# Float16 pairs for layer 1's projections and forgetting-attention logits, with scales from weight bounds gathered in layer 0

## The chip, the core and the metric

One NeuronCore of a Trainium2 chip runs the whole program. The metric is device time in microseconds (us) of one execution, as the median of three. Names of the engines as the profile has them: PE is the matrix engine, PEld its weight loads, DVE the vector engine, ACT the scalar engine, POOL GpSimd, SP the engine whose queue issues all of this kernel's DMAs.

## What is computed

A decoder trunk of two layers over 1024 tokens of width 1024. Layer 0 mixes by causal pooling, layer 1 by forgetting attention; both add a 4-head cross-attention into 256 memory tokens, and both end in an output projection and a LayerNorm.

```python
def mixer_sublayer(x, mem, w_in, w_mem_kv, w_out, main_fn):
    h = x @ w_in                      # 1024 -> 3072: main | mem q | main gate | mem gate
    y_main = main_fn(u_main)
    y_mem = memory_attention(q_mem, mem, w_mem_kv)
    y = concat([y_main * silu(g_main), y_mem * silu(g_mem)])
    return y @ w_out

# layer 1's main_fn; k, v, cum come from one projection of layer 0's output
logits = einsum('bqhd,bkhd->bhqk', qi, k) * FOX_HEAD_DIM ** -0.5
logits = logits + (ci[..., :, None] - cum_k[:, :, None, :])     # causal
p = softmax(logits);  out = einsum('bhqk,bkhd->bqhd', p, v)

x = layer_norm(ALPHA * x + y, ln_g, ln_b)
```

Everything is float32 at the interface: 16 heads of width 64, sequence 1024, in blocks of 128 queries.

## The kernel before

**Three products for one.** To keep float32 accuracy, `hi_lo` (L159) splits an operand into three tiles: `hi`, the value rounded to the 4-byte type fp32r, by ACT (L162); `lo`, the remainder in bfloat16, by DVE (L163); and `top`, the value in bfloat16, by ACT (L164). A product `a*b` is then hi·hi in fp32r plus top·lo and lo·top in bfloat16 (`three`, L153). When `low[0]` is set, in the main loop of the forgetting attention, `gp_hi_lo` (L166) makes a weight's three tiles on POOL instead.

**A slab** (`slab`, L193) is the projection to 128 output channels: two weight pieces of 128x512, each loaded by SP into one of four `raw` buffers and split into two of six `w` buffers (`hi` in one, the pair `lo`/`top` in the other), then 48 matmuls with 512 moving columns (L214): 16 in fp32r and 32 in bfloat16, in two accumulators, each evacuated after its 24th matmul. Layer 0 has 24 slabs and layer 1 has 38.

**Layer 0.** `pool_group(0)`, then `mem_attention` (four slabs of memory queries, after each of which the memory's keys and values of one head are projected by `mem_kv`, L248; then ten rounds, each with one block of memory logits and softmax, and with parts of four gate slabs put between them), then `pool_group(1)` to `(3)`, each with four slabs. `OutProj.rest` (L457) multiplies by `w_out` (L441); `norm` (L481) normalizes 128 rows at a time, and PE transposes them (L294) into `X1`, which `hi_lo` splits into layer 1's `X`.

**Layer 1.** The memory keys (L248) and `mem_attention` again, then `v_first` (L643: the first values and the forget logits, with X as the stationary operand, L657), the forget gates, whose cumulated logs `cum` go through a DRAM line `cumd`, and the main loop `fox` (L873). It goes over 16 heads and, in a head, from the longest block of queries (1024 keys) to the shortest (128). Of each block: POOL masks a part of the row `R` of `cum` (L773); PE makes the logits with two fp32r matmuls for each stretch of up to 512 keys (L191, into three banks `L`); DVE adds `R` and takes the running minimum (L781); ACT takes the exponential (L789); DVE and ACT make the sums' inverse and two float16 halves of the probabilities (L799 to L811); a DMA transposes them (L824), and five rounds later PE multiplies by the values (L833). For the logits, a head's keys lie in one tile as `hi` on 64 partitions and `lo` on the other 64, with a second tile `ws` that has the two swapped by DMA (L716), so that two matmuls over 128 partitions give all four products.

**Order.** PE's order in the main loop is written by hand (`manual_schedule`): `Fill` holds the slabs of the next pairs and gates, and `pump` puts a share of their matmuls between a block's logits and its values, so that slabs are spread evenly over the rounds. All other engines run in the order in which a planner, which follows the text's order as its priority, has put their instructions, each engine one after the other. The planner also gives out the buffers: a load into `raw` waits for the splits that read the buffer's last content, and a split waits for the slab's matmuls that read the `w` buffer's last content.

```python
    def hi_lo(to, src, pinned=False, top=None):
        pin = tc.keep_in_program_order if pinned else lambda ins: ins
        pin(nc.scalar.copy(to.hi, src))
        pin(nc.vector.tensor_tensor(to.lo, src, to.hi.bitcast(F32), ALU.subtract))
        (top or nc.scalar.copy)(to.top, src)
```

## Time and profile before

| | |
|---|---|
| median of three runs | 1219.38 us (1218.32 to 1220.52) |
| the profiled execution | 1218.15 us, of which the profile's span is 1216.4 us |
| granted PE clock | 0.997 of full speed |
| layer 0 up to its output projection | 0 to 330 us of the span |
| output projection, norm and transposes of layer 0 | 330 to 463 us |
| memory keys of layer 1; its memory attention, first values | 463 to 482 us; 482 to 658 us |
| main loop of the forgetting attention | 658 to 1076 us |
| output projection and norm of layer 1 | 1076 to 1216 us |

The stages are read from where each line's matmuls begin and end. Two things are needed to read the rows. A matmul's row gives a mean of 380 ns, which is the time from its start to the modelled arrival of its last result; the next one starts much earlier, so the distance between two starts is what counts, and it comes from a stretch with its count. And a windows row gives, for each engine, busy microseconds with the number of instructions in brackets, then the granted clock, the mean busy share of the 16 DMA engines, and GB/s.

### The profile page before, as it was taken

The numbers are of one execution on the slowest core, as the hardware profiler recorded it, in microseconds if no ns is written. First come the engines' busy times: TensorE is split into PE (matmuls) and PEld (weight loads), VectorE is DVE, ScalarE is ACT, GpSimd is POOL, SyncE is SP. The second block draws the span as 40 slices with busy tenths as digits, with TensorE's granted clock in tenths as the row PEclk, the third lists the DMA queues.
The fourth block names the chain that finished last, engine by engine and source line by source line (L and its number), as shares of the span: only waits on it lengthen the run. The fifth ranks groups of instructions, "written<-read, shape, count | busy, mean of one in ns | idle before, by whom it ended". The sixth has DMA issues, their size and how long they took to land. (4 is left out here: it accounts for less than half of the span.)

```text
span 1216.4 us, 20026 instructions
## 1 busy us (share of the span) xinstructions
PE 1193.7 (98%) x7018; PEld 758.7 (62%) x7018; DVE 793.3 (65%) x1853; ACT 697.4 (57%) x1474; POOL 221.0 (18%) x349
## 2 busy tenths in 40 slices
PE   9999999999999998999999999999999999999996
PEld 4566666555555666667686666666666666665553
DVE  7534676475644457357736888878877888874754
ACT  6556774374542345567533777767776777685220
POOL 4000000000000000000002454544444434640000
PEclk9999999999999999999999999999999999999999
DMA  6232553232452333234517879988887989895340
GB/s 229 84 112 95 122 131 139 95 121 88 164 182 104 111 129 116 70 96 109 159 52 181 162 161 194 181 187 172 182 195 159 193 188 229 222 241 195 132 156 36
DMA packets 267414, 178.68 MB, mean 147 GB/s; under 512 B 212272, under 2 KB 225712, under 8 KB 267312
## 3 DMA queue, kind: packets, MB, share of 16 engines
q1 hardware_dynamic: 267312, 177.40, 56.2%
q8 instruction: 55, 0.90, 0.3%
q14 instruction: 47, 0.39, 0.1%
HBM read 94.97 MB, written 22.61 MB: 97 GB/s over the span
## 5 line engine op out<-in xcount | busy, mean ns | idle before, releaser
L214 PE MATMUL pj<-A,w 128*128 128x512 bf16 (+1 forms) x2928 | 684.7, 390 | 3.1 <-DVE B L724 1.6
L214 PEld LDWEIGHTS <-w 128*128 128x128 bf16 x1984 | 182.3, 98 | 223.8 <-issue 23.3
L214 PEld LDWEIGHTS pj<-A,w 128*128 128x128 f32 x976 | 181.1, 189 | 45.8 <-ACT A L162 2.8
L789 ACT ACTIVATE T<-MK,s 128x512 f32<-128x512 f32 x192 | 111.3, 580 | 41.5 <-DVE s L781 23.6
L811 DVE SCALAR_TENSOR_TENSOR P<-T,s,P 128x512 f16<-128x512 f32 x192 | 111.6, 613 | 34.7 <-ACT P L810 33.4
L163 DVE TENSOR_TENSOR w<-raw,w 128x512 bf16<-128x512 f32 x106 | 75.6, 714 | 83.6 <-PE pj L214 51.5
L810 ACT ACTIVATE P<-T,s 128x512 f16<-128x512 f32 x192 | 103.0, 576 | 46.0 <-ACT T L789 20.1
L441 PEld LDWEIGHTS <-T 128*128 128x128 bf16 x736 | 70.7, 98 | 82.9 <-issue 3.7
L191 PE MATMUL L<-B,B 128*128 128x512 f32 (+3 forms) x384 | 105.8, 381 | 2.2 <-DVE s L781 2.1
L686 POOL MEMSET G<- 128x128 f32 x1 | 0.2, 208 | 581.5 <-ACT MK L164 581.5
L191 PEld LDWEIGHTS L<-B,B 128*128 128x128 f32 x384 | 70.8, 189 | 22.9 <-DVE s L781 4.8
L162 ACT CAST w<-raw 128x512 fp32r<-128x512 f32 x106 | 65.9, 621 | 26.6 <-PE pj L214 14.6
L157 POOL TENSOR_SCALAR w<-raw 128x512 fp32r<-128x512 f32 x108 | 67.3, 629 | 65.0 <-PE pj L214 59.7
L781 DVE CUSTOM_DVE_ANT_0 MK<-L,R 128x512 f32<-128x512 f32 (+3 forms) x128 | 72.5, 566 | 8.7 <-PE L L191 6.9
L164 ACT CAST w<-raw 128x512 bf16<-128x512 f32 x106 | 65.7, 620 | 18.9 <-PE pj L214 18.2
L773 POOL TENSOR_SCALAR_AFFINE_SELECT R<-R 128x128 f32<-128x128 f32 x128 | 41.3, 328 | 174.4 <-DVE s L781 129.4
L168 POOL TENSOR_TENSOR w<-raw,w 128x512 bf16<-128x512 f32 x54 | 69.6, 1288 | 18.7 <-PE pj L214 16.2
L163 DVE TENSOR_TENSOR T<-T,T 128x1024 bf16<-128x1024 f32 x23 | 28.0, 1218 | 52.2 <-ACT T L162 36.9
L833 PE MATMUL O<-T,V 128*64 128x128 f16 (+1 forms) x1152 | 57.6, 220 | 2.7 <-DMA T<-P 2.5
L833 PEld LDWEIGHTS <-V 128*64 128x64 f16 (+1 forms) x1152 | 50.2, 104 | 15.2 <-issue 5.7
L162 ACT CAST T<-T 128x1024 fp32r<-128x1024 f32 x23 | 24.1, 1046 | 60.3 <-DMA T<-y1d 33.9
L441 PE MATMUL pj<-B,T 128*128 128x512 bf16 (+1 forms) x192 | 52.6, 383 | 0.0
(230 smaller groups left out, 1699.3 us busy)
## 6 DMA issues: line engine op xcount, KB each, us to landing
raw<-in_win_dram SPq DMA_DIRECT2D x96, 256.0 KB, 2.8
raw<-in_wout_dram SPq DMA_DIRECT2D x40, 256.0 KB, 2.8
B<-B SPq DMA_DIRECT2D x32, 256.0 KB, 4.2
R<-cumd SPq DMA_DIRECT2D x16, 512.0 KB, 5.0
y0d<-Y SPq DMA_DIRECT2D x12, 512.0 KB, 3.1
T<-y0d SPq DMA_DIRECT2D x12, 512.0 KB, 3.8
T<-y1d SPq DMA_DIRECT2D x11, 512.0 KB, 4.9
raw<-in_wmk_dram SPq DMA_DIRECT2D x16, 256.0 KB, 2.6
```

The source lines that it names most:

```text
L157: nc.gpsimd.tensor_scalar(to, src, 1.0, 1.0, ALU.mult, ALU.mult)
L162: pin(nc.scalar.copy(to.hi, src))
L163: pin(nc.vector.tensor_tensor(to.lo, src, to.hi.bitcast(F32), ALU.subtract))
L168: nc.gpsimd.tensor_tensor(to.lo, src, to.hi.bitcast(F32), ALU.subtract)
L191: nc.tensor.matmul(acc, a, b, start=i == 0, stop=i == len(terms) - 1)
L214: nc.tensor.matmul(accs[n], a[:, k, :], b[:, pc * 4 + k, n * NH : (n + 1) * NH], start=seen[n] == 1, stop=seen[n] == 3 * KT,)
L441: nc.tensor.matmul(accs[a][nh], y, w, start=kt == 8 and i == 0, stop=kt == 7 and i == 2,)
L781: nc.vector.tensor_tensor_reduce(p[:, lo:up], lg, R[:, lo:up], 1.0, top, ALU.add, ALU.min, m[:, n : n + 1])
L789: nc.scalar.activation(e, p[:, lo:up], AF.Exp, bias=top, scale=-1.0, accum_out=sums[:, n, hd % 2, i : i + 1],)
L810: nc.scalar.activation(pair[:, lo:up], e, AF.Copy, scale=r)
L811: nc.vector.scalar_tensor_tensor(pair[:, L + lo : L + up], e, r, pair[:, lo:up], ALU.mult, ALU.subtract)
L833: nc.tensor.matmul(acc[rows, (i % 4) * P : (i % 4) * P + P], v[:, b, 2 * j : 2 * j + (1 if e else 2), :].rearrange("p e d -> p (e d)"), pt ...
```

## The change

**Layer 1's X and its weights become pairs of float16.** `Half` holds `hi` and `lo` in float16 in one buffer, and its `top` is `hi` itself. `scaled_hi_lo` makes them with one ACT instruction (`hi`) and one DVE instruction (`lo`), both with a scale from an SBUF column; on POOL, `gp_scaled_hi_lo` scales the raw piece in place, copies and subtracts. A slab keeps its 48 matmuls, now all in float16. A weight piece takes one `w` buffer where it took two. `X1` takes one of the two `A` buffers; the other becomes `lines`, sixteen float16 rows which hold the queries and keys of the main loop (`qk`), in the place of float32 tiles of the tag `B`. The logits keep their two matmuls for each stretch, now in float16, and the swapped tiles' DMAs move half the bytes.

**Scales.** `sx` follows from the largest values of the norm's gain and offset. `sw` follows from a bound of the weights: before layer 1, each of its 76 pieces of 128x512 and the eight pieces of `wv0` is loaded once more, in layer 0, and ACT sums its absolute values (`look_ahead`). The calls: five pieces after each of layer 0's four memory-query slabs, three in each of the ten rounds of its memory attention, three after each gate slab of pool groups 1 to 3, six at the end of each of these groups; that makes 84. `scales_of`, at the head of layer 0's `OutProj.rest`, then takes the largest sum over all partitions through a DRAM line, and makes the scales and their inverses from powers of two with some twenty small DVE instructions.

**Undoing them.** Projections stay scaled, and what reads them takes the factor from a column: the gate's tanh, the memory queries' split (`q_split`), the memory values' and forgetting values' undo factors, the forget logits. `cum` is divided by the logits' factor before it is stored, and L781 multiplies its sum by `unq`, a column in the place of the constant 1.0.

Layer 0, the memory keys and values, the memory logits, the probabilities and both output projections compute as before.

```diff
+    class Half:
+        def __init__(self, hi, lo):
+            self.hi = self.top = hi
+            self.lo = lo
...
+    def scaled_hi_lo(to, src, sc):
+        nc.scalar.activation(to.hi, src, AF.Copy, scale=sc)
+        nc.vector.scalar_tensor_tensor(to.lo, src, sc, to.hi, ALU.mult, ALU.subtract)
+
+    def gp_scaled_hi_lo(to, src, sc):
+        nc.gpsimd.tensor_scalar(src, src, sc, 1.0, ALU.mult, ALU.mult)
+        gp_copy(to.hi, src)
+        nc.gpsimd.tensor_tensor(to.lo, src, to.hi, ALU.subtract)
...
-    def split_w(src_dram, shape):
+    def split_w(src_dram, shape, sc=None):
         r = raw(shape)
         nc.sync.dma_start(r, src_dram)
+        if sc is not None:
+            to = half_of(wt, shape)
+            (gp_scaled_hi_lo if low[0] else scaled_hi_lo)(to, r, sc)
+            return to
...
+    def look_ahead(n):
+        for k, src in islice(seen_of, n):
+            r = raw(list(src.shape))
+            nc.sync.dma_start(r, src)
+            nc.scalar.activation(r, r, AF.Abs, accum_out=sums[:, k : k + 1])
...
+    def bound_of(m):
+        look_ahead(len(ahead))
+        line = dram.tile([P, 1], F32, name="line")
+        nc.vector.tensor_reduce(m, sums, AX.X, ALU.max)
+        nc.sync.dma_start(line, m)
+        every = raw([P, P])
+        nc.sync.dma_start(every, line.rearrange("p o -> (p o)").partition_broadcast(P))
+        nc.vector.tensor_reduce(m, every, AX.X, ALU.max)
...
+    def q_split(l, to, acc):
+        if not l:
+            return hi_lo(to, acc)
+        nc.scalar.activation(to.hi, acc, AF.Copy, scale=un1)
+        nc.vector.scalar_tensor_tensor(to.lo, acc, un1, to.hi.bitcast(F32), ALU.mult, ALU.subtract)
+        nc.scalar.activation(to.top, acc, AF.Copy, scale=un1)
...
+            look_ahead(5)
...
+                look_ahead(3)
...
+            if X is not None:
+                scales_of(gb)
...
+                if g:
+                    look_ahead(3)
...
+            look_ahead(6)
-        X1 = parts_of(stream, [P, KT, S])
+        X1 = half_of(stream, [P, KT, S])
...
+        lines, line_at = stream([P, 16, S], F16), [0]
...
-            ks, ws = ([xy() for _ in range(2)] for _ in range(2))
+            ks, ws = ([qk() for _ in range(2)] for _ in range(2))
...
-                    nc.scalar.copy(t[own, cols], acc[own, :])
-                    nc.vector.tensor_tensor(t[other, cols], acc[own, :], t[own, cols].bitcast(F32), ALU.subtract)
+                    nc.scalar.activation(t[own, cols], acc[own, :], AF.Copy, scale=QKSCALE)
+                    nc.vector.scalar_tensor_tensor(
+                        t[other, cols], acc[own, :], QKSCALE, t[own, cols], ALU.mult, ALU.subtract,
+                    )
...
-            ws = [parts_of(MK, [P, 4, FW]) for _ in range(2)]
+            ws = [Half(*(MK([P, 4, FW], F16) for _ in range(2))) for _ in range(2)]
...
-                hi_lo(ws[kt // 4][:, kt % 4, :], r)
+                scaled_hi_lo(ws[kt // 4][:, kt % 4, :], r, sw)
...
-                nc.vector.tensor_tensor_reduce(p[:, lo:up], lg, R[:, lo:up], 1.0, top, ALU.add, ALU.min, m[:, n : n + 1])
+                nc.vector.tensor_tensor_reduce(p[:, lo:up], lg, R[:, lo:up], unq, top, ALU.add, ALU.min, m[:, n : n + 1])
```

More of the change, by code (lines that the diff above doesn't have):

```diff
@@ L266, in vals @@
             )
+            if h == MH - 1 and l:
+                nc.vector.tensor_scalar(undo, undo, un1, None, ALU.mult)
             if h == MH - 1:
@@ L319, in mem_attention @@
             q = parts_of(qtile, [P, S])
[L320 removed]
+            run(slab(win[l, 8 + h], X, lambda cols, acc: q_split(l, q[:, cols], acc)))
+            look_ahead(5)
             qs.append(q)
```

78 lines of the change are left out of this document (61 added, 17 removed).

## The prediction

> **What bounds the kernel now.** I read the page first, then the distance between matmuls in the timeline, then busy time by stage, then the groups of the main loop.
>
> ```profile
> span 1216.4 us, 20026 instructions
> PE 1193.7 (98%) x7018; PEld 758.7 (62%) x7018; DVE 793.3 (65%) x1853; ACT 697.4 (57%) x1474; POOL 221.0 (18%) x349
> ```
>
> PE is never long without work, so only fewer or closer matmuls shorten the run. The change keeps their number. What is left is their distance. Two stretches of one slab in layer 0 show it, the first in bfloat16, the second in fp32r (written f32):
>
> ```profile
> 237.37 6.64 PE L214 MATMUL pj<-A,w 128*128 128x512 bf16 x30
> 244.29 3.58 PE L214 MATMUL pj<-A,w 128*128 128x512 f32 x15
> ```
>
> A stretch is its starts and one last matmul, whose mean is 0.38 us in bfloat16 and 0.41 in fp32r (groups below). So the distance is (6.64 - 0.38)/29 = 216 ns and (3.58 - 0.41)/14 = 226 ns: a 4-byte matmul of 512 columns costs 10 ns more, not a multiple. The weight loads differ by more, 98 ns against 189:
>
> ```profile
> L214 PEld LDWEIGHTS <-w 128*128 128x128 bf16 x1984 | 182.3, 98 | 223.8 <-issue 23.3 <-DVE B L713 1.0 <-DVE s L802 0.6
> L214 PEld LDWEIGHTS pj<-A,w 128*128 128x128 f32 x976 | 181.1, 189 | 45.8 <-ACT A L162 2.8 <-POOL w L157 2.4
> ```
>
> 189 ns hide under a matmul of 216, but not under the logits of 256 or 128 columns (108 and 54 ns at the same rate). So the gain lies in the main loop above all. Busy time by stage (us; PE, PEld, DVE, ACT, POOL; clock; DMA share, GB/s):
>
> ```profile
> 64.00:123.00 59.00, 59.00 (x362) 41.32 (x361) 25.92 (x55) 36.92 (x72) 0.00 (x0) 1.00 0.31 95
> 123.00:187.00 64.00, 64.00 (x475) 44.63 (x475) 46.38 (x114) 44.96 (x127) 0.00 (x0) 1.00 0.52 127
> 187.00:330.00 143.00, 143.00 (x658) 81.17 (x656) 85.83 (x131) 74.25 (x124) 0.00 (x0) 1.00 0.34 114
> 330.00:345.00 15.00, 15.00 (x70) 7.96 (x69) 7.09 (x10) 9.17 (x13) 0.00 (x0) 1.00 0.96 324
> 463.00:482.00 19.00, 15.05 (x113) 13.03 (x112) 15.21 (x33) 14.55 (x31) 0.00 (x0) 0.91 0.41 123
> 482.00:658.00 176.00, 175.80 (x1138) 120.80 (x1137) 95.53 (x232) 95.18 (x225) 3.67 (x6) 1.00 0.39 108
> 658.00:1076.00 418.00, 411.50 (x2761) 270.40 (x2760) 337.96 (x973) 300.01 (x698) 194.57 (x320) 1.00 0.88 188
> 973.00:1024.00 51.00, 49.76 (x345) 33.43 (x345) 44.48 (x129) 39.53 (x92) 21.49 (x35) 1.00 0.95 211
> ```
>
> The reader is to see that DVE is at 338 of 418 us, 81%, in the main loop, and ACT at 70% in the stage from 123 to 187, where thirty re-reads go.
>
> **The main loop's matmuls: -16 us.** The groups there:
>
> ```profile
> L214 PE MATMUL pj<-A,w 128*128 128x512 bf16 x864 | 206.6, 380 | 0.0
> L214 PE MATMUL pj<-A,w 128*128 128x512 f32 x433 | 118.7, 405 | 1.6 <-DVE B L724 1.6
> L191 PE MATMUL L<-B,B 128*128 128x512 f32 x160 | 53.8, 433 | 0.0
> L833 PE MATMUL O<-T,V 128*128 128x128 f16 x540 | 35.3, 219 | 0.0
> L191 PE MATMUL L<-B,B 128*128 128x384 f32 x96 | 28.5, 378 | 0.6 <-DVE s L781 0.6
> L191 PE MATMUL L<-B,B 128*128 128x256 f32 x96 | 22.0, 310 | 1.6 <-DVE s L781 1.5
> L833 PE MATMUL O<-T,V 128*64 128x128 f16 x540 | 20.8, 222 | 2.7 <-DMA T<-P 2.5
> L191 PE MATMUL L<-B,B 128*128 128x128 f32 x32 | 8.3, 342 | 0.0
> ```
>
> and one block of values with the slab's matmul after it:
>
> ```profile
> 801.38 0.73 PE L833 MATMUL O<-T,V 128*128 128x128 f16 x10
> 1008.32 1.12 PE L833 MATMUL O<-T,V 128*128 128x128 f16 x20
> 1009.38 0.39 PE L214 MATMUL pj<-A,w 128*128 128x512 bf16 x1
> ```
>
> Float16 at 128 columns steps by (0.73 - 0.22)/9 = 57 ns, the bfloat16 rate. What the loop would need with every matmul at the 16-bit rate: projections (864 + 433) x 0.216 = 280.1; logits 160 x 0.216 + 96 x 0.162 + 96 x 0.108 + 32 x 0.054 = 62.2; values 540 x 0.057 = 30.8, and the 64-wide ones, which run in pairs side by side, half of it, 15.4. Together 388.5 of 418: 29.5 us too much. PE's idle time is 418 - 411.5 = 6.5 of it. Turning between the wide and the paired values costs 1.06 us (1008.32 to 1009.38) less 10 x 0.057 + 5 x 0.057 = 0.86, so 0.2 each for the 30 blocks (1080 values, 36 in a block on average): 6. There remain 17 us for the 4-byte type: 433 x 10 ns = 4 in projections and 13 in the logits' loads. I take 16. The lower bound is 10 ns for each of 817 matmuls, 8; the upper all but the turns, 23.
>
> **Given back to DVE: +3 us.** L781 now reads its factor from a column. The trace shows what a column costs there: 749 ns with the running minimum as one, 683 without.
>
> ```profile
> L781 DVE CUSTOM_DVE_ANT_0 MK<-L,R 128x512 f32<-128x512 f32 x64 | 43.7, 683 | 8.2 <-PE L L191 6.9 <-POOL R L773 0.9
> L781 DVE CUSTOM_DVE_ANT_0 MK<-L,R,s 128x512 f32<-128x512 f32 x16 | 12.0, 749 | 1.1 <-DVE s L781 0.9
> ```
>
> 192 x 66 ns = 13 us more on DVE: 351 of 402, 87%. The busiest stretch of before, 973 to 1024, has 44.48 of 51, also 87%; PE is idle there for 1.24 of 51 us, 2.4%, against 6.5 of 418, 1.6%. 0.8% of 402 is 3 us. Bounds: 0, if the column rides along, and 31, if DVE cannot go beyond its 81% (351/0.81 = 433). I take 3, as the row at 87% was seen at work. The evacuations of queries and keys stay one ACT and one DVE instruction each, the POOL splits three; the swapped tiles' DMAs are halved, and a piece in one `w` buffer lets POOL run further ahead. These I cost at nothing: POOL is at 195 of 418 us, and DMA, at a share of 0.88, loses bytes.
>
> **From 463 to 658: -4 us.** 11 slabs lie here (four memory queries, four gates, three of the first pairs): 176 fp32r matmuls at 10 ns, 1.8. In `v_first` the 64 of 272 columns save the difference of two rows, 19 ns each, 1.2:
>
> ```profile
> L657 PE MATMUL pj<-MK,A 128*128 128x272 bf16 x128 | 15.7, 279 | 0.2 <-DVE B L713 0.2
> L657 PE MATMUL pj<-MK,A 128*128 128x272 f32 x64 | 9.6, 298 | 0.0
> ```
>
> That is 3. From 463 to 482 PE is idle for 4 us, with ACT busy for 14.55 of 19: X1's last four groups each lose one ACT copy there (0.6 us), 2.4 at most; I take 1, bounds 0 and 2.4. Scales from columns make ACT's copies slower by 0.1 us (686 against 585, the rows of L810 and L548 below), 40 of them 4 us in 176, while 16 pieces lose a copy of 0.62: hidden by PE, which has 175.8 us of work there, and less than before without that cover.
>
> **Re-reading weights: +3 us.** A piece costs one load and two ACT instructions. Abs with a sum isn't in the trace; an exponential with a sum is, and four follow each other here:
>
> ```profile
> 146.87 0.47 ACT L345 ACTIVATE P<-L,s 128x256 f32<-128x256 f32 x1 [2.09 <-DVE s L342]
> 147.24 0.19 ACT L345 ACTIVATION_READ_ACCUMULATOR P<-L,s 128x1 f32 x1
> ...
> 148.68 0.63 ACT L162 CAST w<-raw 128x512 fp32r<-128x512 f32 x1
> ```
>
> (148.68 - 146.87)/4 = 0.45 us a pair, where the parts make 0.47 + 0.20: 0.22 overlap. With 0.62 for 512 columns a re-read takes ACT 0.60 us; 0.82 without overlap. Idle ACT time against need: 64 to 123, 22 against 20 x 0.60 = 12; 123 to 187, 19 against 18; 187 to 330, 69 against 20. The middle one fills ACT to 98%, and some of its idle time cannot be used, since ACT stands waiting:
>
> ```profile
> ACT P L345 <- DVE s L342: 9.8, 7, 2.5
> ```
>
> These 10 us leave 9 for 18: 9 over, if nothing moves. But a re-read is not urgent, its turn on ACT can slide into the next stage with 69 idle, and `w` holds two pieces ahead of the one in use, each 24 matmuls or 5 us of PE. Bounds 0 and 9; I take 3, a third of it. Behind a re-read on ACT stand the evacuations of `pj`, and PE waits for those. The price rests on ACT needing no table load for Abs:
>
> ```profile
> L495 ACT ACT_TABLE_LOAD x2 | 2.6, 1283 | 0.0
> L810 ACT ACTIVATE P<-T,s 128x512 f16<-128x512 f32 x80 | 53.2, 686 | 34.3 <-ACT T L789 13.4 <-issue 12.1 <-DVE s L802 4.8
> L548 ACT COPY P<-pj 128x512 f32<-128x512 f32 x14 | 8.2, 585 | 34.1 <-PE pj L214 34.1
> ```
>
> Only the root in `norm` forces one, at 1283 ns; copy, tanh and exponential share one. If Abs were like the root, 23 bursts would load twice, 59 us of ACT. The Trainium skill ("ScalarE: Activation LUTs", section "Table sets: the hidden batching unit") says that abs is in every set as a filler; by it the 59 us are none, and no run here shows it yet.
>
> **The joint at 330: +3 us.** `scales_of` puts into SP's queue a store that waits for DVE's maximum and a load that waits for the store; two landings, and DVE's second maximum waits for them. Behind it on SP stand the first out-projection chunks:
>
> ```profile
> 332.93 0.53 SPq L473 DMA_DIRECT2D T<-y0d  x1
> 338.15 0.53 SPq L473 DMA_DIRECT2D T<-y0d  x1
> ```
>
> and behind it on DVE the `lo` of those chunks, for which PE waits. There is little room: a chunk is 48 matmuls, 10 us, so PE wants at 341 what SP asked for at 333, and DMA is at a share of 0.96 with 324 GB/s. The last six re-reads, 1.5 MB, would add 5 us at that rate if they slip into it. Bounds 0 and 8; I take 3. The scales' twenty small DVE instructions lie in 7.09 of 15 us.
>
> **Sum.** -16 + 3 - 4 + 3 + 3 = -11 on the profiled execution's 1218.15 us, 1207; the median of the runs is 1.2 above it, so 1208.
>
> A rule that would make more of it: the Trainium skill ("TensorE: Matmul & The Clock Gate", section "Back-to-back issue gap") gives some 131 ns for a sustained matmul of 512 columns, and says that N/2.4 + 2.5, which is 216, counts too much. Layer 1's fp32r matmuls would then each gain 95 ns instead of 10. The bfloat16 row, sustained over 30, has 216, so the measurement decides and this has no chance worth naming.
>
> **The rivals.**
>
> *Hidden whole (1195).* Re-reads and scales fit into idle time, and the deeper `w` queue takes PE's waits along: -20 in the loop, -4 before it, nothing given back, 1219.4 - 24. For it: layer 0 has 110 us of idle ACT against 50 of need. Against: the joint has no room.
>
> *DVE is the bound in the loop (1221).* The shorter matmuls end in waits for L781, whose banks are three: at 351/418 = 84% nothing of the 16 is left, and -4 + 6 remain. For it: PE already waits for DVE at the logits (1.5 and 0.6 above). Against: the stretch at 87%.
>
> *The re-reads take the raw buffers (1235).* Four buffers serve weights and re-reads in the order of the text. A weight piece that finds none free comes later by its load (2.8 us), ACT's copy (0.62) and DVE's remainder (0.71), 4.1 in all:
>
> ```profile
> raw<-in_win_dram SPq DMA_DIRECT2D x96, 256.0 KB, 2.8
> L163 DVE TENSOR_TENSOR w<-raw,w 128x512 bf16<-128x512 f32 x106 | 75.6, 714 | 83.6 <-PE pj L214 51.5 <-ACT w L162 30.8 <-PE L L214 0.3
> ```
>
> There are 23 bursts. The gain of 17 (16 - 3 + 4) is gone from the fifth exposed one; at eight, 33 us, it is 1235. For it: the bursts stand in the text before the next slab's pieces. Against: DMA is at a third to a half of its time there, and each burst has a slab of 10 us to pass.
>
> *It does not do what it says:* float16 might stream more slowly than bfloat16. The values' 57 ns exclude it.
>
> **How the numbers follow.** Forecast 0.56, hidden whole 0.17, DVE bound 0.10, raw buffers 0.17; Abs like the root is inside the last. The forecast's own terms give 1199 to 1217. The range, 1193 to 1226, takes in hidden whole, DVE bound and the raw buffers up to five or six bursts; beyond it lies most of the last rival's 0.17. About 0.2% can be told from no change: below 1217 lie the forecast (0.53), hidden whole (0.17) and a little of DVE bound, 0.72; within, 0.08, from the forecast's end and DVE bound; above, 0.20.
>
> **What would show it.** Logits in float16 with loads of 98 ns; the loop from 418 us to about 405; L781 at some 750 and 815 ns and DVE near 87%; 84 Abs in layer 0 with no table load beside the four; PE idle near 341. Wrong would be: a loop as long as before, PE waiting for `raw` or `w` before 330, or a loop under 395 us.

## The result and the profile after

The changed kernel takes 1252.98 us (median of 4 runs, 1251.37 to 1255.45) against 1219.48 (1218.32 to 1220.52): a ratio of 1.0277 with an interval of 1.0256 to 1.0297. It is slower by 33 us, where 11 us less were forecast; the time lies 27 us above the range. The profiled execution, the slowest of the four, has a span of 1253.7 us. From the page of the changed kernel:

```profile
span 1253.7 us, 20190 instructions
PE 1185.7 (95%) x6970; PEld 685.0 (55%) x7018; DVE 811.0 (65%) x1882; ACT 730.3 (58%) x1596; POOL 218.9 (17%) x349
```

PE's recorded busy time fell by 8 us (48 of its 7018 matmuls have no record) and that of the weight loads by 74. But the span is 37 longer: PE waits, where before it hardly did. Where it waits is read from the starts of the first and last matmuls of each stage in the trace (us; "loop" is from the first to the last logits of the forgetting attention):

| kernel | out-projection of layer 0 begins | layer 1 begins | loop | span |
|---|---|---|---|---|
| before | 330.5 | 463.1 | 658.6 to 1073.5, 414.9 | 1216.4 |
| changed | 344.0 | 482.1 | 677.2 to 1109.5, 432.3 | 1253.7 |

So 13.5 us are lost before the out-projection of layer 0, 5.5 in it (138.1 against 132.6), nothing from there to the loop (195.1 against 195.5), 17.4 in the loop, 1.3 behind it. Busy time by stage of the changed kernel (us; PE, PEld, DVE, ACT, POOL; clock; DMA share, GB/s):

```profile
64.00:123.00 59.00, 58.74 (x356) 41.02 (x359) 25.56 (x54) 46.09 (x106) 0.00 (x0) 1.00 0.56 183
123.00:204.00 81.00, 72.99 (x501) 50.98 (x506) 50.75 (x119) 63.36 (x188) 0.00 (x0) 0.96 0.80 215
204.00:344.00 140.00, 138.34 (x619) 78.19 (x629) 81.85 (x126) 93.11 (x188) 0.00 (x0) 1.00 0.49 162
344.00:363.00 19.00, 16.64 (x69) 8.34 (x69) 8.78 (x17) 6.64 (x11) 0.00 (x0) 0.91 0.88 183
...
677.20:1109.50 432.30, 400.56 (x2747) 208.82 (x2746) 344.30 (x973) 298.09 (x693) 180.46 (x305) 0.98 0.80 166
```

In the first two lines the DMA share goes from the 0.31 and 0.52 of before to 0.56 and 0.80. The second line is where layer 0 loses: PE has work for 73 of 81 us, at a clock of 0.96. ACT, which was to be the scarce engine, is idle for 17.6 us; but for 13.8 of them it waits until a re-read has landed, before the Abs of that re-read (L224). From the list of waits of this window (us in total, times, longest):

```profile
DVE s L440 <- ACT P L437: 14.6, 8, 3.0
ACT raw L224 <- DMA raw<-in_wk_dram: 8.2, 3, 2.8
...
ACT raw L224 <- DMA raw<-in_win_dram: 5.6, 5, 1.8
...
PE T L270 <- DMA T<-P: 4.1, 1, 4.1
...
PE T L270 <- DVE Y L460: 2.8, 1, 2.8
```

PE's two waits are in the memory attention, for its turned probabilities and for its values, and not for a weight piece. In the loop PE is idle for 31.7 us. A window of the same work before the change:

```profile
658.60:1073.50 414.90, 408.40 (x2747) 268.22 (x2745) 335.46 (x968) 298.32 (x694) 193.59 (x317) 1.00 0.88 187
```

There it is idle for 6.5. With 2747 matmuls recorded in both, PE's busy time fell by 7.8 us. The groups of the loop, changed kernel:

```profile
L892 DVE CUSTOM_DVE_ANT_0 MK<-L,R,scales 128x512 f32<-128x512 f32 x64 | 47.6, 744 | 7.7 <-PE L L270 5.9 <-POOL R L884 1.5
L892 DVE CUSTOM_DVE_ANT_0 MK<-L,R,s 128x512 f32<-128x512 f32 x16 | 12.9, 807 | 0.9 <-DVE s L892 0.7
L270 PE MATMUL L<-A 128*128 128x384 f16 x96 | 23.7, 329 | 7.3 <-DVE s L892 7.3
L270 PE MATMUL L<-A 128*128 128x256 f16 x96 | 18.6, 276 | 6.4 <-DVE s L892 6.2
L944 PE MATMUL O<-T,V 128*64 128x128 f16 x540 | 21.4, 225 | 15.3 <-DMA T<-P 13.1 <-ACT T L900 2.2
```

The waits have grown at two places: logits wait for the running minimum (L892, which was L781) for 13.9 us where it was 2.1, and values wait for the turned probabilities for 13.1 where it was 2.5. POOL's waits in the loop say what is late ahead of the minimum:

```profile
POOL R L884 <- DVE s L892: 86.8, 38, 5.3
POOL raw L170 <- DMA raw<-in_win_dram: 51.4, 20, 8.2
POOL R L884 <- DVE s L913: 34.1, 16, 4.0
POOL raw L170 <- DMA raw<-in_wv_dram: 26.6, 9, 7.8
POOL raw L170 <- DMA raw<-in_wk_dram: 19.3, 7, 7.1
```

L170 is the scaling of a weight piece in place, the first of the three POOL instructions that split it. It needs nothing but its load, so it stands far ahead in POOL's order, and there POOL stands still for 97 us in 36 waits. Behind it in the same queue is L884, the mask of R, and for that DVE's minimum waits, the first in the list of DVE's waits in the loop. Under it stands the same wait of before:

```profile
DVE MK L892 <- POOL R L884: 26.3, 18, 4.4
```

```profile
DVE MK L781 <- POOL R L773: 2.6, 4, 0.9
```

### The profile page after: what moved, and what is told of

Its sections match the earlier page's. It is cut to its first block, busy times and chain, and to the rows that moved or that the text cites. A ratio compares the mean times of both kernels' runs of the same rounds, so it can differ in the third digit from the quotient of the medians.

```text
span 1253.7 us, 20190 instructions
## 1 busy us (share of the span) xinstructions
PE 1185.7 (95%) x6970; PEld 685.0 (55%) x7018; DVE 811.0 (65%) x1882; ACT 730.3 (58%) x1596; POOL 218.9 (17%) x349
## 5 line engine op out<-in xcount | busy, mean ns | idle before, releaser
L294 PE MATMUL pj<-A,w 128*128 128x512 f16 (+2 forms) x2908 | 674.1, 385 | 8.3 <-DVE A L822 2.9
L294 PEld LDWEIGHTS <-w 128*128 128x128 f16 (+1 forms) x2592 | 249.7, 98 | 291.8 <-issue 14.7
L270 PE MATMUL L<-A 128*128 128x512 f16 (+3 forms) x384 | 86.0, 327 | 14.1 <-DVE s L892 13.9
L892 DVE CUSTOM_DVE_ANT_0 MK<-L,R,scales 128x512 f32<-128x512 f32 (+3 forms) x128 | 80.3, 627 | 9.5 <-PE L L270 5.9
L224 ACT ACTIVATE raw<-raw 128x512 f32<-128x512 f32 (+1 forms) x84 | 51.2, 610 | 57.5 <-DMA raw<-in_wv_dram 20.1
L294 PEld LDWEIGHTS pj<-A,w 128*128 128x128 f32 x368 | 69.0, 190 | 20.1 <-ACT A L186 3.1
L944 PE MATMUL O<-T,V 128*64 128x128 f16 (+1 forms) x1152 | 59.1, 224 | 15.3 <-DMA T<-P 13.1
L270 PEld LDWEIGHTS <-A 128*128 128x128 f16 x384 | 37.2, 98 | 58.6 <-issue 18.7
L944 PEld LDWEIGHTS <-V 128*64 128x64 f16 (+1 forms) x1152 | 52.2, 106 | 29.4 <-DMA T<-P 13.3
L172 POOL TENSOR_TENSOR w<-raw,w 128x512 f16<-128x512 f32 x54 | 63.3, 1173 | 3.7
L884 POOL TENSOR_SCALAR_AFFINE_SELECT R<-R 128x128 f32<-128x128 f32 x128 | 39.9, 317 | 131.1 <-DVE s L892 88.9
L170 POOL TENSOR_SCALAR raw<-raw,scales 128x512 f32<-128x512 f32 x54 | 38.9, 721 | 123.6 <-DMA raw<-in_win_dram 73.5
L892 DVE CUSTOM_DVE_ANT_0 MK<-L,R,s 128x512 f32<-128x512 f32 (+1 forms) x64 | 41.0, 641 | 25.3 <-POOL R L884 23.7
```

The source lines that it names most:

```text
L172: nc.gpsimd.tensor_tensor(to.lo, src, to.hi, ALU.subtract)
L224: nc.scalar.activation(r, r, AF.Abs, accum_out=sums[:, k : k + 1])
L270: nc.tensor.matmul(acc, a, b, start=i == 0, stop=i == len(terms) - 1)
L294: nc.tensor.matmul(accs[n], a[:, k, :], b[:, pc * 4 + k, n * NH : (n + 1) * NH], start=seen[n] == 1, stop=seen[n] == 3 * KT,)
L892: nc.vector.tensor_tensor_reduce(p[:, lo:up], lg, R[:, lo:up], unq, top, ALU.add, ALU.min, m[:, n : n + 1])
L944: nc.tensor.matmul(acc[rows, (i % 4) * P : (i % 4) * P + P], v[:, b, 2 * j : 2 * j + (1 if e else 2), :].rearrange("p e d -> p (e d)"), pt ...
```

## The experiments

Three theories stood at first. A: POOL's scaling in place blocks the masks. B: the factor read from a column makes DVE too slow. C: the re-reads take layer 0's time. All edits are against the changed kernel unless another is named. A time without a ratio is one run. The last three columns are from the profiled execution. What stands behind the loop is not the same in all of them (144 us in the changed kernel, 151 in e2 and e5, 154 in e12), so loops are compared with loops and not with times. The loop of e10 is 3.5 us below that of the changed kernel with no edit in the loop: differences of that size say little.

| kernel | time | ratio to before (interval) | out-projection begins | layer 1 begins | loop |
|---|---|---|---|---|---|
| e1 POOL scales into `w` | 1246.57 | 1.0219 (1.0197 to 1.0241) | 345.9 | 484.9 | 419.0 |
| e2 constant factor | 1269.74 | | 347.2 | 486.4 | 434.8 |
| e3 no re-reads | 1236.92 | 1.0138 (1.0122 to 1.0155) | 331.4 | 464.2 | 432.6 |
| e4 re-reads elsewhere | 1265.81 | | 345.1 | 490.2 | 433.0 |
| e5 no load, constant factor | 1236.17 | | 332.3 | 467.9 | 420.8 |
| e6 no sum, six rounds | 1245.36 | | 340.9 | 476.4 | 426.6 |
| e7 own buffers | 1237.96 | | 344.8 | 480.9 | 418.0 |
| e8 all constants | 1217.11 | | 331.0 | 463.9 | 414.5 |
| e9 a quarter of each piece | 1247.28 | | 334.9 | 473.3 | 432.4 |
| e10 POOL's queue | 1268.11 | | 358.3 | 497.3 | 428.8 |
| e11 six rounds, more buffers | 1223.75 | | 330.3 | 462.9 | 417.2 |
| e12 no remainder on DVE | 1215.00 | | 330.5 | 463.1 | 402.5 |
| e13 one remainder on POOL | 1214.44 | 0.9949 (0.9934 to 0.9963) | 330.9 | 464.1 | 412.8 |
| e14 values' sum on POOL too | 1219.43 | 0.9988 (0.9978 to 0.9998) | 331.1 | 463.7 | 416.7 |
| e15 before, edits of e14 | 1225.01 | 1.0036 (1.0024 to 1.0048) | 331.9 | 465.7 | 419.4 |
| e16 exponentials in SBUF | 1240.07 | | 330.5 | 463.1 | 439.5 |
| e17 three banks | 1218.49 | | 329.9 | 465.6 | 415.4 |
| e18 remainder without high half | 1216.03 | | 331.4 | 463.8 | 414.3 |

**e1: POOL scales into another buffer.**

```diff
-        nc.gpsimd.tensor_scalar(src, src, sc, 1.0, ALU.mult, ALU.mult)
-        gp_copy(to.hi, src)
-        nc.gpsimd.tensor_tensor(to.lo, src, to.hi, ALU.subtract)
+        scaled = wt(list(src.shape), F32)
+        nc.gpsimd.tensor_scalar(scaled, src, sc, 1.0, ALU.mult, ALU.mult)
+        gp_copy(to.hi, scaled)
+        nc.gpsimd.tensor_tensor(to.lo, scaled, to.hi, ALU.subtract)
```

> Edit: in the main loop POOL scales a weight piece into a buffer of the tag w and no longer in place, so that its first instruction waits for a w buffer as the old split did; all else as in the changed kernel. Theory A (the in-place scaling needs nothing but its load, so it stands early in POOL's order and waits there for the load, 97 us in 36 waits, with the masks of R behind it and DVE's L781 behind those): the main loop falls from 432 us to 405-412, POOL's waits for loads fall under 20 us, DVE's waits for R from 26 to under 8 us, and the time to about 1228-1235. Theory B (L781's column of 66 ns makes DVE the bound): the main loop stays within 4 us of 432. Layer 0 stays 13 us longer than before in both.

Now the first instruction needs a free `w` buffer as well, and takes its place in the order where the work is wanted. The waits of POOL for loads are gone from the loop's list, and DVE's for the mask are two fifths of what they were:

```profile
DVE MK L893 <- POOL R L885: 10.5, 10, 2.4
```

The loop falls by 13.3 us to 419.0. A is shown, but the loop is still 4 us longer than before, and misses the 405 to 412 expected. The time falls by 6.4 us only, since layer 1 begins 2.8 us later here and the profiled execution of the changed kernel was its slowest. The edit also frees the `raw` buffer after the first POOL instruction instead of the third; that share was not tried alone.

**e2: the factor of L892 as a constant 1.0** (leaves the factor out).

> Edit: L781's line reads the constant 1.0 in place of the column unq (the logits' factor is left out); all else as in the changed kernel. Theory B: the main loop falls by 10 us or more. Theory A: L781 gets 66 ns shorter in each of its 192 instructions, 13 us of DVE, and the main loop falls by no more than 4 us, since DVE is waiting for R.

The loop is 434.8: B falls. The column does cost 61 and 58 ns an instruction (744 and 807 against 683 and 749, the rows above and the prediction's), 192 of them some 11 us of DVE, and none of it shows in the loop. Nor does it without POOL's waits: e5 has the constant and the POOL edit, and its loop is 420.8 against 419.0 in e1.

**e3: no re-reads and no trip through memory**; the bound of the weights is a constant (leaves the bound out).

```diff
+    ahead = ahead[:0]
...
-        look_ahead(len(ahead))
-        line = dram.tile([P, 1], F32, name="line")
...
+        nc.vector.memset(m, 40.0)
```

> Edit: no weight is read a second time; the bound is the constant 40.0 (the bound is left out). Theory C (the re-reads and the trip of their maximum cost layer 0 its 19 us): the out-projection of layer 0 begins at 330-332 us in place of 344, layer 1 begins at 463-466 in place of 482, the main loop stays at 428-435, and the time is about 1234. Rival D (the new splits of X1 and the buffers, not the re-reads, delay the joint): layer 1 begins at 468 or later.

Layer 0 is back where it was, layer 1 begins at 464.2, and the loop does not care. C is shown: 17.9 us at that point, about half of the loss. In the window that lost most, DMA's share is back at 0.54, and PE at work for all but 0.4 us:

```profile
123.00:204.00 81.00, 80.56 (x556) 54.92 (x562) 56.15 (x128) 49.96 (x136) 0.00 (x0) 1.00 0.54 133
```

The next six ask what of a re-read costs.

**e4: the re-reads moved** out of the memory attention into the pool groups (`look_ahead(6)` and `look_ahead(10)` there).

> Edit: the thirty re-reads between the ten rounds of layer 0's memory attention go to the pool groups (six after each gate slab, ten at each group's end). Theory C1 (the stage is too full for them: ACT at 98%, SP's queue behind): the stage from the first memory logits to the next pool group shrinks from 76 to 64-66 us, and the three pool groups together grow by 0-4 us. Rival C2 (any place is as dear, since each re-read costs its load and its 0.6 us of ACT): what the stage gains is lost in the groups, and the out-projection begins at 342-345 as now.

The memory attention has its old pace again, and the groups lose it instead, the out-projection too: no place takes them for nothing.

**e5: no load.** A memset by POOL stands for each re-read's load, ACT's sums stay, and so does the trip through memory; with the POOL edit of e1 and a constant factor (the bound and the factor are left out).

> Edits, in stages that do not overlap: (1) layer 0's re-reads take a raw buffer and ACT's sum as now, but POOL fills the buffer and nothing is loaded (the bound is the constant 40.0, the loads are left out); (2) the main loop has POOL's scaling into a w buffer, and L781's line the constant 1.0 (the logits' factor is left out). Theory C-ACT (ACT's 51 us of sums and the buffers are what layer 0 pays for): the out-projection of layer 0 begins at 341 us or later. Theory C-load (the loads, their wait on ACT and their turn in SP's queue): it begins before 336. In the main loop, theory B2 (with POOL's wait gone, DVE's 12 us of columns are what is left): it falls from 419 to 410 or less. Rival L (the way from logits to transposed probabilities is longer than the five rounds it is given): it stays at 415-420.

**e6: loads without sums.** The re-reads' loads stay, Abs goes; with the POOL edit, and values six rounds behind the logits instead of five (the bound is left out).

> Edits, in stages that do not overlap: (1) layer 0's re-reads are loaded into raw buffers, but ACT does not sum them (the sums are left out; the bound is the constant 40.0); (2) the main loop has POOL's scaling into a w buffer, and the values come six rounds after their logits in place of five. C-ACT: the out-projection of layer 0 begins before 335; C-load: at 338 or later. In the main loop, rival L: it falls from 419 to 412 or less, and PE's waits for the transposed probabilities go; B2: it stays at 416-421.

These two answer each other: with sums and no loads layer 0 loses 1.8 us, with loads and no sums 10.4. So the loads alone can cost most of the 13.5 us. By which way they do it is less clear. ACT takes its instructions in order, and from 64 to 345 us it waits 49 us, in 33 waits, for re-reads to land before their Abs; in e6, where no Abs is left, it waits 25 us for weight pieces before their splits, a wait that is not in the list of before. In e5 such waits, for POOL's memset instead of a load and for weight pieces, make 16.5 us. With loads gone the out-projection takes 135.6 us, 3.0 more than before: that is the trip, with what the sums add.

**e7: buffers of their own** for 68 of the 84 re-reads; with the POOL edit.

> Edit: the first 68 re-reads of layer 0 go to four buffers of their own (the tag W, free until then), the last sixteen to raw; POOL's scaling into a w buffer as in e1. Theory C-raw (the four raw buffers are what weights and re-reads fight for): the out-projection begins at 331-336 us. Rival C-ACT or C-load: 341 or later, as with the raw buffers (345.9).

Free of the weights' buffers the re-reads only start sooner: the first stage, from 64 to 123 us, now has the loss (the first logits of the memory attention start 13.5 us late), with DMA at 253 GB/s:

```profile
64.00:123.00 59.00, 55.13 (x308) 36.46 (x307) 23.47 (x51) 50.58 (x128) 0.00 (x0) 0.97 0.79 253
```

So taking the re-reads out of the four `raw` buffers gains nothing. But ACT is busy for 50.6 of these 59 us, where it was 36.9 before, and PE waits most for ACT's copies (3.2 us in two waits): this loss is not simply that of the changed kernel in another place.

**e9: a quarter of each piece** is loaded and summed (three quarters of the weights are left out of the bound).

> The changed kernel with one edit: a re-read loads and sums only a quarter of its piece (64 KB instead of 256), so the 84 issues, the buffers and their order stay while the bytes and most of ACT's sums go; three quarters of the weights are left out of the bound, which is multiplied by four. Theory C-bytes: the 13.5 us that layer 0 lost before its out-projection are the transfer time that the re-reads put between the weights' own pieces; with a quarter of it the out-projection begins at 331 to 336 instead of 344.0, and the time falls by 8 to 13 us, to 1240 to 1245. Rival C-issue: it is the 84 places in SP's queue and the turns of the buffers; then it begins at 341 or later and the time stays within 3 us of 1253. The loop stays at 432 in either case.

84 issues as before, a quarter of the bytes: 9.1 of the 13.5 us are gone. So the 84 issues and turns of buffers are not what costs most. The bytes are the likely reason, but ACT's Abs got shorter as well (309 ns against 629, medians), and ACT still waits 40 us for re-reads.

```profile
123.00:204.00 81.00, 77.78 (x543) 52.90 (x541) 52.98 (x122) 57.85 (x194) 0.00 (x0) 1.00 0.65 157
```

**e10: issued from POOL's queue** instead of SP's.

> The changed kernel with one edit: the 84 re-reads are issued from POOL's queue instead of SP's; bytes, buffers and sums stay, and POOL has nothing else to do in layer 0. Theory C-queue: the weights' pieces come late because they stand in SP's queue behind a re-read that waits for its buffer; then the out-projection begins at 331 to 336 instead of 344.0 and the time falls by 8 to 13 us. Rival C-bytes: the transfers themselves are in the way; then it begins at 341 to 346 and the time stays within 4 us of 1253.

It is worse than either theory expected, the out-projection at 358.3. So leaving SP's queue gains nothing by itself; what made it worse by another 14 us was not followed, and with it this run does not tell what SP's order costs.

**e8: all scales constants**, with the POOL edit of e1 (bounds and re-reads are left out).

> Edit: all scales are constants of the program (the bounds of weights and norm and the re-reads are left out), so that no instruction reads a factor from a column; POOL's scaling goes into a w buffer. Layer 0 as before (331 us, layer 1 at 464). Theory B2: the main loop takes 405-410 us and the time is about 1210, under the kernel before. Rival L: the main loop takes 415-420 and the time is 1220-1224.

This is the change with nothing but its float16 left, and it shows best what became of the gain. Its loop:

```profile
656.80:1071.30 414.50, 395.71 (x2747) 207.95 (x2746) 333.39 (x973) 296.88 (x693) 182.71 (x310) 1.00 0.84 174
```

PE is busy for 395.7 us against 408.4 before: 12.7 of the 16 us are there. But it is idle for 18.8 against 6.5, 12.3 more, and the loop has the old length. PE's first wait is now the one for the turned probabilities:

```profile
PE O L905 <- DMA T<-P: 9.0, 6, 2.4
PE L L233 <- DVE s L853: 4.6, 8, 0.8
```

The matmuls were not all that held the rounds to 415 us. What ACT and DVE wait for each other is in e8 nearly what it was before: DVE for ACT's high half 31.6 us in 53 waits (before 33.4 in 56), ACT for the minimum 25.1 in 30 (before 22.8 in 26). The rhythm of these two did not change with faster matmuls; that is what to expect if they, and not PE, set the pace, though it does not prove it.

What does? The rest works on e8. A round is logits (PE), running minimum (DVE), exponential with its sum (ACT), reciprocal (DVE), high half (ACT), remainder (DVE), and the transposing DMA.

**e11: values six rounds behind, the turned probabilities in ten idle buffers** instead of six.

> The kernel with all scales constant (bounds and re-reads left out; its loop was 414.5 us, with 14 us of PE waiting for the turned probabilities before values) and two edits: values six rounds after their logits instead of five, and the turned probabilities in the ten idle buffers of X's projections instead of T's six. Theory D-delay: what ate the float16 gain in the loop is the way from the logits to the turned probabilities, which takes a fixed time while the five rounds got shorter; with a sixth round and the buffers for it the loop falls to 400 to 407 us. Rival D-throughput: DVE, with 333 us of work in 414 and its turns with ACT, passes no more rounds in a given time; then waits move from the values to the logits and the loop stays at 412 or above.

No wait for turned probabilities is left, and the loop is 417.2: PE waits for the minimum instead.

```profile
PE L L233 <- DVE s L853: 14.2, 12, 2.4
```

More delay is not the answer; e6, which had it without the buffers, has a loop of 426.6 and says the same.

**e12: the remainder left out**, with zeros by POOL in its place.

```diff
-                nc.vector.scalar_tensor_tensor(pair[:, L + lo : L + up], e, r, pair[:, lo:up], ALU.mult, ALU.subtract)
+                nc.gpsimd.memset(pair[:, L + lo : L + up], 0.0)
```

> The kernel with all scales constant (bounds and re-reads left out), and one edit: the low half of the probabilities, which DVE takes as a remainder after ACT's high half, is left out, and POOL fills its place with zeros. Some 70 us of DVE's 333 go from the loop, and one step of the way from logits to values moves to an engine that is not late. Theory D-throughput: the loop falls from 414.5 to 395 to 405 us, near the matmuls' own 384 and the turns. Theory D-delay: most of the rounds' way is left, so only part of the 14 us of waiting for values goes, and the loop stays at 408 or above.

```profile
656.40:1058.90 402.50, 393.24 (x2747) 206.27 (x2746) 239.55 (x787) 294.33 (x694) 250.57 (x500) 1.00 0.86 180
```

The loop falls by 12 us to 402.5, with PE busy for 393.2 of it. Here nearly the whole of float16 is seen in PE's busy time: 408.4 to 393.2, 15 us. The end came only 2 us earlier than in e8: the last out-projection then waits for its rows, whose load stands in SP's queue behind weights that come through four `raw` buffers.

```profile
PE L L497 <- ACT T L189: 8.4, 1, 8.4
```

**e13, e14, e15: less work for DVE, nothing left out of it.** e13 is e8 with the remainder of the turned value projections on POOL (six in the loop, 1282 ns each), and the last out-projection asks for its first rows before its last eight weights. e14 moves the second half of the values' evacuation as well, to an ACT copy and a POOL addition. e15 makes the edits of e14 in the kernel before.

```diff
-        nc.vector.scalar_tensor_tensor(lo, u, sc, hi, ALU.mult, ALU.subtract)
+        if low[0]:
+            nc.gpsimd.tensor_scalar(u, u, sc, 1.0, ALU.mult, ALU.mult)
+            nc.gpsimd.tensor_tensor(lo, u, hi, ALU.subtract)
...
-            nc.vector.scalar_tensor_tensor(oc, acc[own, :], un[own], oc, ALU.mult, ALU.add)
+            if hd // 2 < 7:
...
+                nc.scalar.activation(part, acc[own, :], AF.Copy, scale=un[own])
+                nc.gpsimd.tensor_tensor(oc, oc, part, ALU.add)
```

> The kernel with all scales constant (bounds and re-reads left out; loop 414.5 us) and two edits: the remainder of the turned value projections (1282 ns, six times in the loop) is taken by POOL instead of DVE, and the last out-projection asks for its first chunk before the last eight weights. Theory D-throughput (DVE passes 80% of the time and paces the loop): 7.7 us less DVE work take 7.7/0.80, some 9 us, off at most, so the loop is 404 to 411 us and the time 1206 to 1214. Rival D-pattern (the waits between ACT and DVE pace it, not the amount): the loop stays at 412 to 417.

> As e13, and the second half of the values' evacuation goes from DVE to an ACT copy and a POOL addition (another 21 us off DVE, 20 more on ACT). D-throughput: DVE's 333 us fall to some 305, the loop becomes the matmuls' own with their turns, 398 to 405 us, and the time is 1200 to 1207. Rival D-pattern, or ACT as the next bound (298 + 20 of 400): 410 us or more.

> The kernel before, with the edits of e14: 28 us of DVE's work in the loop go to ACT and POOL, the matmuls stay fp32r and bfloat16. If DVE paced the loop of before as well, its 414.9 us fall to 404 to 410 and the time to 1208 to 1214; the distance to e14, 4 to 10 us, is then what float16 is worth without that bound. If PE paced the loop of before, as the prediction had it, the loop stays at 413 to 417 and the time within 3 us of 1219.

The loops of e14 and e15:

```profile
655.50:1072.20 416.70, 396.59 (x2747) 207.42 (x2746) 309.31 (x939) 314.54 (x721) 232.31 (x350) 1.00 0.83 175
```

```profile
661.20:1080.60 419.40, 406.96 (x2715) 268.03 (x2745) 311.52 (x934) 315.77 (x722) 241.85 (x357) 1.00 0.84 185
```

24 us less for DVE and 18 more for ACT, and both loops are longer, by 2.2 and 4.5 us (e14 against e8, e15 against before). So the amount of DVE's work alone does not pace it; an amount that ACT and DVE share is not excluded, since ACT got most of what DVE lost. For e15 neither expectation came true: its 419.4 us lie above both. e13, which gives ACT nothing, gains 1.7 in the loop, too little to tell. It is 0.5% faster than before; it has the constants of e8, so it is no full replacement for the change.

**e16: the exponentials in SBUF** instead of two PSUM banks. **e17: three banks** for them, and two for the logits.

> The kernel with all scales constant (bounds and re-reads left out; loop 414.5 us) and one edit: the exponentials of the first fourteen heads go to the idle SBUF buffers of X's projections instead of two PSUM banks; every instruction, its size and its order stay. Theory E-banks (exponential, sum, high half, remainder pass through two banks, and a round of two parts fills both, so the rounds cannot overlap): the waits of the exponentials for the remainders go, and the loop falls to 398 to 407 us, the time to 1201 to 1212. Rival D-pattern (ACT and DVE wait for each other's results whatever the buffers): the loop stays at 411 or above. If the exponential or the remainder takes over 60 ns longer in SBUF, the loop may lose what the banks give.

> As the kernel with all scales constant, but the exponentials (and all other users of these banks) have three PSUM banks instead of two, and the logits two instead of three. Theory E-banks: the exponentials' waits for the remainders shrink from 17 us to under 8 and the loop to 402 to 411 us, unless the logits, now with two banks, wait for the running minimum instead; PE's waits for DVE's minimum, 4 us in all, then say by how much. Rival D-pattern: the loop stays at 412 or above without such waits.

In e16 the remainder takes 745 ns on the mean; in e8 it took 614 (the two groups, e16 first):

```profile
L885 DVE SCALAR_TENSOR_TENSOR P<-B,s,P 128x384 f16<-128x384 f32 (+1 forms) x168 | 120.0, 745 | 26.0 <-ACT P L884 25.4
```

```profile
L883 DVE SCALAR_TENSOR_TENSOR P<-T,s,P 128x384 f16<-128x384 f32 (+1 forms) x188 | 109.4, 614 | 32.9 <-ACT P L882 31.6
```

168 times 131 ns are 22 us, and the loop is 25 longer. ACT's waits for the remainder, 17.2 us in e8, are gone as expected, but with the longer remainder the run does not tell what the banks are worth. POOL's masks slowed as well (466 against 328 ns). In e17 ACT's waits for the remainder shrink from 17.2 to 8.9 us as expected, and those for the minimum grow from 25.1 to 63.0:

```profile
ACT T L861 <- DVE s L853: 63.0, 75, 2.6
...
ACT T L861 <- DVE P L883: 8.9, 16, 1.1
```

A third bank alone does not shorten the loop: with less waiting for the banks, ACT stands waiting for DVE. But the logits gave a bank up for it, and PE's waits for the minimum went from 4.6 to 14.8 us, so the run does not exclude the banks altogether.

**e18: the remainder subtracts a tile of zeros** (leaves the subtraction of the high half out).

> The kernel with all scales constant (bounds and re-reads left out; loop 414.5 us) and one edit: DVE's remainder of the probabilities subtracts a tile of zeros instead of ACT's high half, so that it has the same size and reads as much but no longer waits for ACT (what is left out is the subtraction of the high half). Theory F-link: DVE's 32 us of waits for the high half pace the loop together with its work; DVE gains most of them, the loop falls to 396 to 406 us as it did without the remainder, with DVE busier than 80%, and the time to 1199 to 1214. Rival D-amount: the same DVE work passes in the same time, other waits of DVE grow instead, and the loop stays at 410 or above.

```profile
DVE P L885 <- ACT P L884: 31.6, 53, 1.1
```

This is e8's wait to the tenth (31.6 us in 53). DVE does not read the high half any more and still waits for it, so the edit took no wait away and tells nothing of the link. Whether the order comes from the bank that both read or from the tile that both write was not tried.

## Why the prediction was wrong

The forecast was 11 us less, and the profiled span grew by 37.3: 48.3 us off. Of these, 30.4 are in the loop (17.4 more, where -16 and +3 make 13 less), 10.5 before the out-projection of layer 0, 2.5 in it, 3.6 from there to the loop and 1.3 behind it. The steps that failed most are three: a saving of PE's subtracted from the length of the loop, POOL's instructions put at nothing, and re-reads priced by ACT's work alone.

**"The main loop's matmuls: -16 us."** The size was right, the place wrong. PE's busy time in the loop fell by 12.7 us in e8 and by 15 in e12; the loads of the logits take 98 ns, as forecast:

```profile
L270 PEld LDWEIGHTS <-A 128*128 128x128 f16 x384 | 37.2, 98 | 58.6 <-issue 18.7
```

The term was subtracted from the length of the loop, on the ground that "PE is never long without work". In e8 the saving is there and the loop is the old one (414.5 against 414.9), so a second limit lay within 1 or 2% of the first. What the runs point to are the turns of ACT and DVE within a round. They are at 298 and 335 us of 415, each waiting for the other's last result, so neither looks full. e12 (without the remainder, 12 us less of loop) shows that the remainder lies on that path, and e16 (22 us more for it, 25 more of loop) agrees; e11 and e14 exclude the delay and DVE's amount alone, e17 a gain from one bank more. Which of the waits within the round sets the pace stays open after e18.

**"These I cost at nothing": POOL's three instructions.** They cost 13.3 us of loop (e1). POOL's total was held against the loop (195 of 418 us), and the total did not grow (180 of 432). What counts is what its first instruction waits for. The split of before had its first instruction wait for a `w` buffer; the scaling in place waits for a load alone, and was put where the load had not landed. "A piece in one `w` buffer lets POOL run further ahead" was noted, and read as good.

**"Given back to DVE: +3 us."** The 60 ns an instruction came as forecast, but DVE went from 81 to 80% and not to 87, and e2 finds no cost of the column in the loop. The upper bound of this term, 31 us, came from a loop of 433 if DVE could not go beyond 81%, and the loop came out at 432.3 with DVE at 80%. That is chance: in e2 DVE is busy for 10 us less, 77%, and the loop is no shorter. e1's loop is 4.5 us above e8's; e5, with the factor constant and the other scales in columns, is above it too (420.8). That remainder was not taken apart.

**"Re-reading weights: +3 us"** came out as +13.5. The price was made for ACT's work, and that part is right: an Abs with its sum is followed by ACT's next instruction after 0.62 us, where 0.60 was said, and e6 without the sums gains only 3 us:

```profile
L224 ACT ACTIVATE raw<-raw 128x512 f32<-128x512 f32 (+1 forms) x84 | 51.2, 610 | 57.5 <-DMA raw<-in_wv_dram 20.1 <-DMA raw<-in_wk_dram 19.2 <-DMA raw<-in_win_dram 17.2
...
L590 ACT ACT_TABLE_LOAD x2 | 2.6, 1283 | 0.0
```

Table loads are four as before, two of them the root's. The Trainium skill ("ScalarE: Activation LUTs", section "Table sets: the hidden batching unit") has abs in every set; the trace agrees, with 84 Abs and no further load. What was not priced are the loads: 84 pieces, 76 of them of 256 KB, into stages whose DMA share of 0.31 and 0.52 was read as room. Loads without sums cost 10.4 us (e6), a quarter of the bytes 4.4 (e9). And the prediction let a re-read's turn on ACT "slide into the next stage"; but ACT stands in order, and the row above has 56.5 us in which it waited for a re-read to land, with the exponentials of the memory attention among the work behind it. How the 13.5 us divide between the transfer itself, the order in SP's queue and ACT's waiting stays open.

**"The joint at 330: +3 us"** came out as 5.5: 3.0 for the trip (e5), as said, and the rest for the last re-reads. The rest is gone without loads and without sums (135.6 and 135.5 us, e5 and e6) and stays with a quarter of the bytes (138.4, e9), so it is not the 5 us of transfer that the prediction named. Its wait is as described, DVE's second maximum behind the line's way through memory:

```profile
DVE s L239 <- DMA raw<-line: 9.0, 1, 9.0
```

**"From 463 to 658: -4 us"** came out as -0.4, with constants -2.6. `v_first` gained the 1.2 us expected (22.4 against 23.6), the stage of the keys 0.8 (18.2 against 19.1).

**The rivals.** "The re-reads take the raw buffers" had the right place; its mechanism is not borne out, since re-reads with buffers of their own cost as much (e7). Its 1235 holds only the loss of layer 0. "DVE is the bound in the loop" was right that nothing of the 16 us would be left, and wrong in DVE's amount as its reason. The argument against it, a stretch at 87%, showed that DVE can be busier, not that the rounds can be shorter. The two together, with POOL's waits, which no rival had, make the 33 us.

**The range.** 1193 to 1226 was narrower than the terms' own bounds. At their upper ends these make -8 + 31 - 3 + 9 + 8 = +37, some 1256, and the measured 1253 lies below that. The range took in the rivals one at a time; here several terms failed together.

## What to carry to other kernels

Before a saving on the busiest engine is subtracted from the time, ask which wait ends second: two engines at 70 and 80% that take turns can be a limit as near as one at 98%. Their waits for each other, 33 us of DVE's for ACT before the change, are a place to look. An instruction that needs only its load can be put early by a planner, and it then blocks what stands behind it on an engine that runs in order (here POOL's scaling, and it seems ACT's Abs), so look at what each new instruction waits for before looking at what it costs. A read that nobody waits for is not free either: loads without any work on them cost layer 0 10 us (e6), and fewer bytes cost less (e9).

## What the runs showed of the hardware

The same remainder takes DVE 745 ns with its source in SBUF and 614 in PSUM, and POOL's mask goes from 328 to 466 ns in the same run (e16); whether the two slow each other was not tried. A re-read issued by POOL takes it 546 ns (median), and layer 0 lost 14 us more than with SP's issues (e10). Windows in which PE waits for some microseconds have a lower granted clock: 0.96 from 123 to 204 us and 0.91 from 344, where before the change windows without such waits had 1.00. In the second, PE waits once for 2.3 us; the four matmuls of 512 columns behind that wait start 427 ns apart, and those after them 216 again. So that wait cost more than its length.
